# Rotary positions loaded by one transfer on the weights' queue instead of four on GpSimd's

## The chip, the core and the metric

The kernel runs on one core of one Trainium2 chip. The metric is the device time of one execution in microseconds. The engines are named as the profile names them: PE is TensorE (PEld its weight loads), DVE is VectorE, ACT is ScalarE, POOL is GpSimd, and SP issues transfers. An engine name with a q behind it (SPq, POOLq) is that engine's instruction queue.

## What is computed

One decoder layer for 256 tokens of width 2048, in float32: a norm of the input, one wide projection, causal attention with low-rank queries and keys (16 heads), a short gated convolution beside it, two output projections merged by gates, an output projection, a norm and the residual. What the change touches is the rotary table, which turns integer positions into a cosine and a sine for each of 32 frequencies:

```python
def _rope_tables(positions):
    inv_freq = ROPE_THETA ** (-jnp.arange(0, ROPE_DIM, 2, dtype=jnp.float32) / ROPE_DIM)
    ang = positions.astype(jnp.float32)[..., None] * inv_freq
    return jnp.cos(ang), jnp.sin(ang)
...
h = _rmsnorm(x, pre_norm_g)
proj = jnp.einsum('bsd,de->bse', h, w_in)
(q_a, c_kv, k_rope, z_mla, ...) = jnp.split(proj, cuts, axis=-1)
q  = jnp.einsum('bsr,re->bse', _rmsnorm(q_a, q_a_norm_g), w_q_b)
kv = jnp.einsum('bsr,re->bse', _rmsnorm(c_kv, kv_a_norm_g), w_kv_b)
q_rope = _apply_rope(q_rope, cos, sin); k_rope = _apply_rope(k_rope, cos, sin)
```

The positions are 256 consecutive integers from a start below 1024. The rotary parts are first used for the keys and the first heads' queries, after q_a, c_kv and k_rope have been projected.

## The kernel before

**Weights.** All weights come through SP's queue as a list of units, in the order in which TensorE uses them (`plan`, filled by `add`). A unit is one transfer, mostly 1 MB. The first eight (`u_qa`) hold two slices of the transposed input and of the q_a weights each, 768 KB; then come four units of c_kv's weights (`u_ckv`), one of k_rope's (`u_kr`), and those of the gates z, the heads and the output projections. `load_raw` issues a unit's transfer (line 157), the first three units in two transfers each. Units go into three rotating buffers named `raw`, except the fourth to the sixth, which borrow room from `cv_f` and `at_f` so that six units can be on the way at once (`early`, line 298). A unit that reuses a `raw` buffer is issued when the unit before it in that buffer has been split.

**Splitting.** Every float32 operand is split into a high and a low part so that TensorE can multiply at its faster type: ScalarE rounds the high part (`whi`, line 237) and VectorE subtracts it from the source to get the low part (`wlo`, line 238). The eight first units need a scaled copy of the input too, made by ScalarE (line 338) and VectorE (line 341). A product is three matmuls: high by high, and the two crossed ones. All matmuls go through line 88 in program order; those of transposes through line 91.

**Order at the start.** TensorE multiplies q_a (eight units, `qa` in the profile), c_kv (four units, `ckv`), k_rope (`kr`), then the first gate units (`z`), between which the normalised q_a and c_kv are transposed (`lt_qa`, `lt_ckv`, line 484). Beside that, the other engines compute:

- the input norm: ScalarE sums squares of the token-major input (line 351) and GpSimd takes the inverse root with a power (line 358);
- the norms of q_a and c_kv, in the same way, each with its own power on GpSimd and its own scaling on ScalarE (line 475);
- the rotary table, in `tables()`.

**The table.** `tables()` is a generator that is advanced at four places. Its first part loads the positions: four transfers on GpSimd's queue (line 396), each spreading 64 of the 256 positions over 32 partitions, so that the tile `ta_i` holds 128 partitions by 64 positions (frequency by partition). GpSimd converts them (line 407) and reduces the angles exactly into plus or minus pi by 35 small instructions in a row (lines 402 and 405), each reading what the one before wrote. The second part, advanced after the first c_kv unit, clamps the angle on VectorE (line 429) and takes sine and cosine on ScalarE (lines 431 and 432). The third, advanced after the second c_kv unit, copies the results in 32 pieces into `cos_t` and `sin_t` on GpSimd (line 439). The last fixes signs on VectorE (line 442).

**What sets the order.** A planner orders instructions by a timing model, but those inside `keep_in_program_order` keep their written order on their engine. The table's instructions on GpSimd, its clamp and its sine and cosine are kept so, and so are all matmuls. Each engine runs its queue strictly in order: an instruction that waits holds all behind it.

Of the kernel before, what the change touches and what calls it, by code (L numbers as in the profile page):

```python
# [13 lines left out]
I32 = mybir.dt.int32  # L14
# [4 lines left out]
P = 128  # L19
S = 256  # L20
# [20 lines left out]
SQ = S // 4  # L41
# [41 lines left out]
def tile_layer(ctx: ExitStack, tc: tile.TileContext, xw, x, pos, pvec, post_g, wc, wz, wcv, wkr, wqk, wqr, wv, cwr, wsq, out):  # L83
    nc = tc.nc
# [23 lines left out]
    def add(ap, width=UNIT):  # L108
        plan.append((ap, width))
        return len(plan) - 1  # L110


    u_qa = [add(xw[i], 2 * XW) for i in range(KD // 2)]
# [36 lines left out]
    def load_raw(i):  # L150
        ap, w = plan[i]
        t = early.get(i)
        if t is None:
            t = wpool.tile([P, UNIT], F32, name=f"raw{i}", tag="raw", bufs=3)
        cuts = {0: (S, XW, 2 * XW), 1: (0, XW, 2 * XW), 2: (0, XW, 2 * XW)}.get(i, (0, w))
        for a, b in zip(cuts[:-1], cuts[1:]):
            nc.sync.dma_start(out=t[:, a:b], in_=ap[:, a:b])
        raws[i] = t
        if i == u_ckv[1]:
            tc.keep_in_program_order(nc.sync.dma_start(out=x_tok, in_=x))  # L160

    def split_unit(i):
        t, w = raws.pop(i), plan[i][1]
        parts = []
        if i == u_kr:
            t = t[:, :w].rearrange("p (k c) -> p k c", k=KD)
            for h in range(2):
                both = wpool.tile([P, HALF], F32R, name=f"whi{i}_{h}", tag="whi", bufs=5)
                both = both[:, :].rearrange("p (k j c) -> p k j c", k=KD // 2, j=2)
                ks = slice(h * KD // 2, (h + 1) * KD // 2)  # L170
                split_act(both[:, :, 0], both[:, :, 1], t[:, ks])
                parts.append(both.rearrange("p k j c -> p k (j c)"))
            splits[i] = parts
            return
        if i <= u_qa[-1]:

            hi, lo = (wpool.tile([P, HALF], F32R, name=f"{o}{i}", tag=o, bufs=5) for o in ("whi", "wlo"))
            for j in range(2):
                k, o = 2 * i + j, j * XW
                src = x_first if k == 0 else t[:, o : o + S]  # L180
                split_scaled(x_both, src, k)
                split_act(hi[:, j * R : (j + 1) * R], lo[:, j * R : (j + 1) * R], t[:, o + S : o + XW], True)
            splits[i] = [(hi, lo)]
            return
        for h in range(0, w, HALF):
            n = min(HALF, w - h)
            if u_out[3, 0] <= i < u_out[3, 3]:
                hi, lo = (op.tile([P, HALF], F32R, name=f"w{o}{i}_{h}") for o in ("hi", "lo"))
            else:
                hi = wpool.tile([P, HALF], F32R, name=f"whi{i}_{h}", tag="whi", bufs=5)  # L190
                lo = wpool.tile([P, HALF], F32R, name=f"wlo{i}_{h}", tag="wlo", bufs=5)
            split_act(hi[:, :n], lo[:, :n], t[:, h : h + n])
            parts.append((hi, lo))
        splits[i] = parts

    def ahead(i, raw=3, split=1):
        while done["raw"] < min(i + raw, len(plan)):
            load_raw(done["raw"])
            done["raw"] += 1
        while done["split"] < min(i + 1 + split, len(plan)):  # L200
            while done["raw"] <= done["split"]:
                load_raw(done["raw"])
                done["raw"] += 1
            split_unit(done["split"])
            done["split"] += 1

    def take(i):
        ahead(i)
        parts = splits.pop(i)

        def piece(j, n):
            o = j * n
            h, o = o // HALF, o % HALF
            return parts[h][0][:, o : o + n], parts[h][1][:, o : o + n]

        return piece

    def bank(name, tag="mm", bufs=4):
        return psum.tile([P, 512], F32, name=name, tag=tag, bufs=bufs)
# [30 lines left out]
    def col(name, k=0):  # L250
        o, _ = PV[name]
        return pv[:, o + k : o + k + 1]
# [47 lines left out]
    def temp(name, shape=(P, S), dt=F32, bufs=2, tag=None):  # L300

        tag, n = tag or name.rstrip("0123456789_"), shape[-1]
        if n % LINE == 0:
            return bp.tile(list(shape), dt, name=name, tag=tag, bufs=bufs)
        return bp.tile([P, -(-n // LINE) * LINE], dt, name=name, tag=tag, bufs=bufs)[:, :n]
# [83 lines left out]
        nc.vector.tensor_tensor(dst, dst, r_x[:, :], op=ALU.mult)  # L389


    def tables():

        pi = temp("ta_i", (P, SQ), I32, 1)
        for q in range(4):
            nc.gpsimd.dma_start(
                out=pi[32 * q : 32 * q + 32, :], in_=pos[:, SQ * q : SQ * (q + 1)].to_broadcast([32, SQ])
            )
        y, n1, n2, r = (temp(f"ta_{n}", (P, SQ), bufs=1) for n in "ymnr")

        def scale(*a, **kw):
            tc.keep_in_program_order(nc.gpsimd.tensor_scalar(*a, **kw))

        def minus(*a):
            tc.keep_in_program_order(nc.gpsimd.tensor_tensor(*a, op=ALU.subtract))

        tc.keep_in_program_order(nc.gpsimd.tensor_copy(y[:, :], pi[:, :]))
        scale(r[:, :], y[:, :], col("freq"), None, op0=ALU.mult)

        def less(r, n, c):  # L410

            scale(y[:, :], n[:, :], c, None, op0=ALU.mult)
            minus(r[:, :], r[:, :], y[:, :])

        inv = 1.0 / (2.0 * math.pi)
        big, small = 1.5 * 2.0**38, 1.5 * 2.0**23
        scale(y[:, :], r[:, :], inv, None, op0=ALU.mult)
        scale(n1[:, :], y[:, :], big, big, op0=ALU.add, op1=ALU.subtract)
        minus(n2[:, :], y[:, :], n1[:, :])
        scale(n2[:, :], n2[:, :], small, small, op0=ALU.add, op1=ALU.subtract)  # L420
        for w, c in TERMS:
            less(r, (n1, n2)[w], c)
        scale(n1[:, :], r[:, :], inv, small, op0=ALU.mult, op1=ALU.add)
        scale(n1[:, :], n1[:, :], small, None, op0=ALU.subtract)
        for c in COARSE:
            less(r, n1, c)
        yield
        lim = float(np.nextafter(np.float32(math.pi), np.float32(0)))
        tc.keep_in_program_order(nc.vector.tensor_scalar(r[:, :], r[:, :], lim, -lim, op0=ALU.min, op1=ALU.max))
        nc.vector.scalar_tensor_tensor(y[:, :], r[:, :], -1.0, r[:, :], op0=ALU.mult, op1=ALU.max)  # L430
        tc.keep_in_program_order(nc.scalar.activation(n2[:, :], r[:, :], AF.Sin))
        tc.keep_in_program_order(nc.scalar.activation(n1[:, :], y[:, :], AF.Sin, bias=hpi[:, :], scale=-1.0))
        yield

        for o in range(4):
            for q in range(4):
                to, ti = slice(32 * o, 32 * o + 32), slice(32 * q, 32 * q + 32)
                for dst, src in ((cos_t, n1), (sin_t, n2)):
                    tc.keep_in_program_order(nc.gpsimd.tensor_copy(dst[to, SQ * q : SQ * (q + 1)], src[ti, :]))
        yield  # L440
        tc.keep_in_program_order(
            nc.vector.tensor_scalar(sin_t[:, :], sin_t[:, :], col("sign"), None, op0=ALU.mult)
        )
        yield
# [11 lines left out]
    def latent_products(pss, k, w, wk):  # L456
        cols = [x_both[:, k, o : o + P] for o in (0, P, S, S + P)]
        wh, wl_ = w(wk, R)
        for i, ws, first, last in ((0, wh, True, False), (2, wh, False, False), (0, wl_, False, True)):
            for t in range(NT):  # L460
                matmul(
                    pss[t][:, :], cols[i + t], ws, start=first and k == 0, stop=last and k == KD - 1
                )
# [13 lines left out]
    def latent_turn(name, both, g, tags):  # L477
        f = lat_f[name]
        for j2 in range(2):
# [5 lines left out]
            for j in range(2):  # L485
# [4 lines left out]
                )  # L490

    table_parts = tables()
    next(table_parts)
    ps_q = [bank(f"qa{t}") for t in range(NT)]
    for i in range(KD // 2):
        ahead(u_qa[i], raw=3 + len(early), split=0)
        w = take(u_qa[i])
        for j in range(2):
            latent_products(ps_q, 2 * i + j, w, j)
# [584 lines left out]
```

## Time and profile before

| | |
|---|---|
| median of 3 runs | 1038.01 us (1038.0 to 1038.07) |
| profiled execution | 1039.19 us |
| its span | 1037.4 us |
| granted TensorE clock | 0.998 |
| busy: PE, DVE, ACT, POOL | 1027.2, 682.3, 526.6, 181.0 us |
| SP's queue (q1) | 197.54 MB |
| GpSimd's queue (q0) | 29.38 MB |

The times in the profile start at the span's first instruction, and the span is 1.8 us shorter than the execution's time. In a row of the timeline the first number is the start, the second the length (of a merged group, from the first start to the last end), then engine, line, operation, what is written and read, and how many; the bracket tells how long the engine stood idle before it and what ended the wait. In the DMA view the last number is the time from a transfer's issue to its landing, and the share of a queue is that of all 16 DMA engines' time. In the chain by time the rows are start, length and what ran.

### The profile page before, as it was taken

The numbers are of one execution on the slowest core, as the hardware profiler recorded it, in microseconds if no ns is written. First come the engines' busy times: TensorE is split into PE (matmuls) and PEld (weight loads), VectorE is DVE, ScalarE is ACT, GpSimd is POOL, SyncE is SP. The second block draws the span as 40 slices with busy tenths as digits, with TensorE's granted clock in tenths as the row PEclk, the third lists the DMA queues.
The fourth block names the chain that finished last, engine by engine and source line by source line (L and its number), as shares of the span: only waits on it lengthen the run. The fifth ranks groups of instructions, "written<-read, shape, count | busy, mean of one in ns | idle before, by whom it ended". The sixth has DMA issues, their size and how long they took to land.

```text
span 1037.4 us, 12723 instructions
## 1 busy us (share of the span) xinstructions
PE 1027.2 (99%) x4694; PEld 856.3 (83%) x4694; DVE 682.3 (66%) x954; ACT 526.6 (51%) x733; POOL 181.0 (17%) x345
## 2 busy tenths in 40 slices
PE   9999999999999999999999999999999999999996
PEld 7888888888888888888888888888888888888885
DVE  7579777787687786767777785564465455455562
ACT  7767555555555455554554564444334434443551
POOL 7620321114211232212313120020010001002000
PEclk9999999999999999999999999999999999999999
DMA  8745766568565685757676766565555566558642
GB/s 323 304 175 215 232 213 234 193 222 295 190 250 202 219 282 189 272 210 243 236 262 200 261 228 212 183 228 198 203 203 209 197 203 236 181 191 331 235 165 82
DMA packets 41952, 231.04 MB, mean 223 GB/s; under 512 B 7521, under 2 KB 8225, under 8 KB 18977
## 3 DMA queue, kind: packets, MB, share of 16 engines
q1 hardware_dynamic: 29808, 197.54, 53.9%
q0 software_dynamic: 11648, 29.38, 8.5%
q10 hardware_dynamic: 432, 3.29, 0.8%
q8 instruction: 37, 0.61, 0.2%
q14 instruction: 27, 0.21, 0.1%
HBM read 214.48 MB, written 11.53 MB: 218 GB/s over the span
## 4 chain that ended last, share of the span: by engine, by line
PE 98%; DMA 1%; DVE 0%; ACT 0%; SPq 0%; DVEq 0%; issue 0%
PE cv L88 34%; PE sq L88 34%; PE z L88 8%; PE out L88 8%; PE qn L88 2%; PE kn L88 2%; PE vv L88 2%; PE ckv L88 2%; PE qa L88 2%; PE sc L88 1%; PE qr L88 1%; PE o L88 1%; DMA raw<-xw_dram 1%; PE kr L88 0%; DVE og L971 0%; PE lt_qa L91 0%
## 5 line engine op out<-in xcount | busy, mean ns | idle before, releaser
L238 DVE TENSOR_TENSOR wlo<-raw,whi 128x1024 fp32r<-128x1024 f32 (+1 forms) x370 | 441.1, 1198 | 284.1 <-ACT whi L237 273.9
L237 ACT ACTIVATE whi<-raw 128x1024 fp32r<-128x1024 f32 (+1 forms) x372 | 382.9, 1035 | 396.2 <-PE sq L88 180.5
L88 PE MATMUL cv<-whi,x_both 128*128 128x512 f32 x1024 | 321.1, 389 | 0.0
L88 PEld LDWEIGHTS cv<-whi,x_both 128*128 128x128 f32 x1024 | 192.3, 188 | 39.2
L88 PE MATMUL cv<-wlo,x_both 128*128 128x512 f32 x512 | 199.5, 390 | 0.0
L88 PE MATMUL sq<-whi,x_both 128*128 128x512 f32 x512 | 158.3, 389 | 0.0
L88 PEld LDWEIGHTS sq<-whi,x_both 128*128 128x128 f32 x512 | 96.1, 188 | 19.9
L88 PEld LDWEIGHTS cv<-wlo,x_both 128*128 128x128 f32 x512 | 96.2, 188 | 19.0
L88 PE MATMUL sq<-wlo,x_both 128*128 128x512 f32 x256 | 99.6, 389 | 0.0
L88 PE MATMUL z<-whi,x_both 128*128 128x512 f32 x256 | 80.6, 390 | 0.0
L88 PE MATMUL sq<-whi,at_both 128*128 128x512 f32 x256 | 79.5, 389 | 0.0
L88 PE MATMUL sq<-whi,cv_both 128*128 128x512 f32 x256 | 79.4, 389 | 0.0
L88 PE MATMUL out<-whi,m_both 128*128 128x512 f32 x256 | 78.9, 389 | 0.0
L319 POOL DMA_DIRECT2D far<-sg x32 | 17.5, 555 | 312.2 <-DVE sg L312 238.6
L319 POOL DMA_DIRECT2D far<-via x64 | 35.4, 560 | 195.1 <-DVE via L312 194.7
L88 PEld LDWEIGHTS sq<-wlo,x_both 128*128 128x128 f32 x256 | 48.0, 188 | 10.0
L88 PEld LDWEIGHTS z<-whi,x_both 128*128 128x128 f32 x256 | 48.1, 188 | 9.9
L88 PEld LDWEIGHTS sq<-whi,at_both 128*128 128x128 f32 x256 | 48.0, 188 | 9.9
L88 PEld LDWEIGHTS out<-whi,m_both 128*128 128x128 f32 x256 | 48.0, 188 | 9.9
L88 PEld LDWEIGHTS sq<-whi,cv_both 128*128 128x128 f32 x256 | 48.0, 188 | 9.9
L88 PE MATMUL z<-wlo,x_both 128*128 128x512 f32 x128 | 49.8, 389 | 0.0
L88 PE MATMUL sq<-wlo,at_both 128*128 128x512 f32 x128 | 49.8, 389 | 0.0
(214 smaller groups left out, 1128.0 us busy)
## 6 DMA issues: line engine op xcount, KB each, us to landing
raw<-wsq_dram SPq DMA_DIRECT2D x80, 1024.0 KB, 4.7
raw<-wcv_dram SPq DMA_DIRECT2D x64, 1024.0 KB, 5.8
raw<-wz_dram SPq DMA_DIRECT2D x16, 1024.0 KB, 4.7
raw<-wqk_dram SPq DMA_DIRECT2D x8, 1024.0 KB, 5.1
cw<-cwr_dram POOLq DMA_DIRECT2D x24, 256.0 KB, 6.2
raw<-wc_dram SPq DMA_DIRECT2D x4, 1024.0 KB, 9.9
raw<-wv_dram SPq DMA_DIRECT2D x4, 1024.0 KB, 4.7
far<-via POOLq DMA_DIRECT2D x64, 48.0 KB, 3.3
```

Source lines behind the costliest of these rows:

```text
L88: return tc.keep_in_program_order(nc.tensor.matmul(*a, **kw))
L237: a = nc.scalar.activation(hi, src, AF.Copy)
L238: b = nc.vector.tensor_tensor(lo, src, hi.bitcast(F32), op=ALU.subtract)
L319: tc.keep_in_program_order(nc.gpsimd.dma_start(out=f[i], in_=m))
```

## The change

The positions are laid out in the input array as the tile needs them: 128 rows of 64 integers, each group of 64 positions repeated over 32 rows, instead of one row of 256. One transfer on SP's queue loads all of them, issued directly behind the sixth unit of the plan and ahead of the seventh, and kept in that place in program order. The four transfers on GpSimd's queue are gone. The tile is made ahead of `tables()`, and the generator's first part is now advanced after the first six units have been issued. What is computed from the tile is unchanged.

As compiled, every engine has the same instructions in the same order as before, except that GpSimd loses the four transfers and SP's queue gains one.

```diff
@@ load_raw
         raws[i] = t
+        if i == u_qa[5]:
+            tc.keep_in_program_order(nc.sync.dma_start(out=tables_pi, in_=pos))
         if i == u_ckv[1]:
             tc.keep_in_program_order(nc.sync.dma_start(out=x_tok, in_=x))
@@ tables
+    tables_pi = temp("ta_i", (P, SQ), I32, 1)
+
     def tables():
 
-        pi = temp("ta_i", (P, SQ), I32, 1)
-        for q in range(4):
-            nc.gpsimd.dma_start(
-                out=pi[32 * q : 32 * q + 32, :], in_=pos[:, SQ * q : SQ * (q + 1)].to_broadcast([32, SQ])
-            )
+        pi = tables_pi
@@ the q_a stage
     table_parts = tables()
-    next(table_parts)
     ps_q = [bank(f"qa{t}") for t in range(NT)]
     for i in range(KD // 2):
         ahead(u_qa[i], raw=3 + len(early), split=0)
+        if i == 0:
+            next(table_parts)
         w = take(u_qa[i])
@@ the arrays made on the host
-        "pos": arr(positions).reshape(1, S),
+        "pos": np.repeat(arr(positions).reshape(4, SQ), 32, axis=0),
```

## The prediction

> **What bounds the kernel now.** I read the page's busy shares first, then the chain by time for the opening, the DMA view, and the timeline of each engine up to 60 us.
>
> ```profile
> span 1037.4 us, 12723 instructions
> ...
> PE 1027.2 (99%) x4694; PEld 856.3 (83%) x4694; DVE 682.3 (66%) x954; ACT 526.6 (51%) x733; POOL 181.0 (17%) x345
> ```
>
> TensorE is the bound and is busy for 99% of the span. So a saving elsewhere buys almost nothing, and whatever makes TensorE wait costs its full length.
>
> ```profile
> 1.64 6.58 DMA raw<-xw_dram
> ...
> 9.33 19.38 PE qa L88 x84
> 28.71 21.76 PE ckv L88 x96
> ```
>
> The chain by time: a transfer releases the second unit's work, and from 9.33 us on it is TensorE alone: qa, then ckv (four units of four k's), then kr. The change touches the inputs of the table that ScalarE and VectorE make beside this stretch.
>
> ```profile
> at_f<-xw_dram SPq DMA_DIRECT2D x1, 768.0 KB, 11.8
> ...
> ta_i<-pos_dram POOLq DMA_DIRECT2D x4, 8.0 KB, 6.1
> ```
> ```profile
> 1.80 2.16 POOL L396 DMA_DIRECT2D ta_i<-pos_dram  x4
> ...
> 4.76 0.43 SPq L157 DMA_DIRECT2D at_f<-xw_dram  x1
> ...
> 7.03 4.37 SPq L157 DMA_DIRECT2D raw<-xw_dram  x2
> ...
> 9.93 0.24 POOL L407 CAST ta_y<-ta_i 128x64 f32<-128x64 int32 x1 [5.03 <-DMA ta_i<-pos_dram]
> ...
> 10.27 1.02 POOL L402 TENSOR_SCALAR ta_r<-ta_y,pv 128x64 f32<-128x64 f32 x1
> ...
> 13.44 0.60 POOL L405 TENSOR_TENSOR ta_n<-ta_y,ta_m 128x64 f32<-128x64 f32 x1
> ...
> 15.91 0.86 POOL L405 TENSOR_TENSOR ta_r<-ta_r,ta_y 128x64 f32<-128x64 f32 x1
> ...
> 16.86 0.42 POOL L402 TENSOR_SCALAR ta_y<-ta_m 128x64 f32<-128x64 f32 x1
> ...
> 24.61 1.22 POOL L402 TENSOR_SCALAR ta_y<-ta_n 128x64 f32<-128x64 f32 x1
> ...
> 29.52 1.10 POOL L402 TENSOR_SCALAR ta_m<-ta_r 128x64 f32<-128x64 f32 x1
> ...
> 30.70 0.38 POOL L402 TENSOR_SCALAR ta_m<-ta_m 128x64 f32<-128x64 f32 x1
> ...
> 33.35 0.32 POOL L405 TENSOR_TENSOR ta_r<-ta_r,ta_y 128x64 f32<-128x64 f32 x1
> ```
>
> GpSimd's range reduction: a cast at 9.93, then 35 dependent instructions from 10.27 to 33.35 + 0.32 = 33.67. It is the only long thing between the positions and the sine.
>
> ```profile
> 33.94 0.26 ACT L431 ACTIVATE ta_n<-ta_r 128x64 f32<-128x64 f32 x1 [3.69 <-DVE ta_r L429]
> ...
> 34.66 2.01 ACT L237 ACTIVATE whi<-raw 128x1024 fp32r<-128x1024 f32 x2
> ...
> 41.50 4.18 ACT L237 ACTIVATE whi<-raw 128x1024 fp32r<-128x1024 f32 x5
> ```
> ```profile
> 33.95:45.65 11.70, 11.70 (x53) 9.68 (x52) 6.60 (x14) 11.51 (x18) 3.94 (x5) 1.00 0.54 212
> ```
>
> ScalarE already stands idle for 3.69 us before the sine (L431), which is kept in program order. Behind it stand the splits of ckv's third unit (34.66), the squares of the input norm and, at 41.50, the splits of ckv's fourth unit. From 33.94 to 45.68 (41.50 + 4.18) ScalarE has no gap to speak of (the stretch's row: length, then busy us of PE, PEld, DVE, ACT and POOL; ACT 11.51 of 11.70), so a late sine moves all of this by the same amount.
>
> **The change part by part.**
>
> *The four GpSimd issues go* (2.16 us from 1.80). Behind them stand only mask instructions, needed by the first scores, long after; GpSimd idled 5.03 us for the positions anyway. Worth nothing.
>
> *Their packets leave the first 10 us of DMA.*
>
> ```profile
> q1 hardware_dynamic: 860, 2.96, 94.9%
> q0 software_dynamic: 128, 0.03, 2.8%
> ```
>
> Between 4 and 12 us (the DMA view of that stretch) the four transfers took 2.8% of 8 us = 0.22 us. The second unit may land up to that much earlier, so TensorE may start at 9.1 for 9.33: a gain of 0 to 0.22 us, which the next step swallows if TensorE waits later.
>
> *One issue on SP's queue behind the sixth unit.* SP issues it at about 5.2 (4.76 + 0.43), in the gap before the seventh unit's at 7.03; about 0.4 us, free. In the compiled program the transfers take eight completion counters in turn, so one more makes the seventh unit's issue wait for the second unit's first piece. The chain above has that piece land at 1.64 + 6.58 = 8.2. The seventh unit is queued behind units that land up to 16.56, so an issue at 8.2 is not late; with the positions' 128 rows ahead of it, it lands some 0.2 later, and TensorE takes it up only after 22 us (five units of 2.72 us from 9.33; 2.72 is half of 21.76/4). Free.
>
> *The positions land later: this carries the price.* At 5.2 us the queue holds most of six units. The sixth (at_f) landed 4.76 + 11.8 = 16.56, and the positions stand behind it. Their own 0.22 us are balanced by the 0.22 taken out ahead. I take 16.56 + 0.15 (landing to cast in the profile: the last of the old four, issued near 3.46, landed by 9.8, cast 9.93) = 16.7 for the cast, not 9.93: 6.8 us late. Bounds: 16.5 (with the sixth unit) and 17.2 (0.5 us of their own).
>
> *How much of 6.8 us reaches the sine.* The pace of the 35 instructions depends on what VectorE does beside them:
>
> ```profile
> 10.97 0.47 DVE L341 SCALAR_TENSOR_TENSOR x_both<-raw,pv,x_both 128x256 fp32r<-128x256 f32 x1
> 11.36 0.68 DVE L238 TENSOR_TENSOR wlo<-raw,whi 128x512 fp32r<-128x512 f32 x1
> ...
> 17.62 0.54 DVE L341 SCALAR_TENSOR_TENSOR x_both<-at_f,pv,x_both 128x256 fp32r<-128x256 f32 x1
> 18.08 0.72 DVE L238 TENSOR_TENSOR wlo<-at_f,whi 128x512 fp32r<-128x512 f32 x1
> ...
> 23.62 3.16 DVE L238 TENSOR_TENSOR wlo<-raw,whi 128x512 fp32r<-128x512 f32 x3
> ...
> 28.03 2.49 DVE L238 TENSOR_TENSOR wlo<-raw,whi 128x1024 fp32r<-128x1024 f32 x2 [1.25 <-ACT whi L237]
> ```
>
> Slow pace: from 10.27 to 16.86, 7 instructions, 0.94 us each; each that overlaps a 0.68 us subtraction (L238) ends just after it. Quick pace: from 16.86 to 24.61, 14 instructions, 0.55 each, two for each VectorE pair, which stretches a little (0.47 to 0.54, 0.68 to 0.72). From 24.61 to 30.70, beside the wide subtractions, 7. Then, with VectorE waiting, 7 from 30.70 to 33.67: 0.43 each.
>
> In the changed kernel the first starts at 16.7 + 0.34 (10.27 - 9.93) = 17.04, so 7.6 us are left up to 24.61. The quick pace set in where a two-input subtraction (L405) alternates with a scale (L402); the first four (three scales, then a subtraction) are not such, and in the profile the step from first to fourth took (13.44 - 10.27)/3 = 1.06 each. So four take 4.2 us (to 21.3) and the rest of the stretch holds 3.3/0.55 = 6: ten done by 24.61, 17 by 30.70. The other 18 run at 0.43 us while VectorE and ScalarE both wait for them: 7.7 us, ready at 38.4 instead of 33.67, so the sine is 4.7 us late. Ends: all quick, 13 + 7 done, 15 left, 37.15 (3.5 late); all slow, 8 + 7, 20 left, 39.3 (5.6 late).
>
> The Trainium skill, "SBUF — State Buffer", section "Who interferes with whom", says that a VectorE instruction with two SBUF inputs and a GpSimd one that reads SBUF hold one port pair by turns, the second to issue blocked until the first ends. By that rule a GpSimd instruction loses at most the rest of one subtraction and then has its turn, two fit each VectorE pair from the start, and the sine would be 3.5 us late. The rows agree only from 16.86 on; from 10.27 the turns went one to a pair.
>
> *What of 4.7 us reaches TensorE.*
>
> ```profile
> 39.20 0.87 PEld L88 LDWEIGHTS ckv<-whi,x_both 128*128 128x128 f32 x4
> ...
> 42.58 1.22 DVE L238 TENSOR_TENSOR wlo<-raw,whi 128x1024 fp32r<-128x1024 f32 x1 [0.26 <-ACT whi L237]
> ...
> 45.55 0.41 PEld L88 LDWEIGHTS ckv<-wlo,x_both 128*128 128x128 f32 x2
> ```
>
> The third ckv unit's high part is split by 34.66 + 1.0 = 35.66 and taken at 39.20: slack 3.5. The fourth unit's low part is ready at 43.80 and taken at 45.55: slack 1.75, less 0.05 from an end to a start, 1.7. That is the least, so TensorE ends 4.7 - 1.7 = 3.0 us later: about 1.2 us of wait at the third unit, the rest at the fourth. The possible 0.22 us at the start is inside this, since the sine's time does not hang on TensorE. Nothing later gives it back: TensorE has no other gap.
>
> *What is late next.*
>
> ```profile
> 42.40 0.70 POOL L358 TENSOR_TENSOR r_qa<-v_qa,mhalf 128x2 f32<-128x2 f32 x1 [0.94 <-DVE v_qa L471]
> ...
> 57.83 0.69 POOL L358 TENSOR_TENSOR r_ckv<-v_ckv,mhalf 128x2 f32<-128x2 f32 x1
> ...
> 58.80 1.27 ACT L475 ACTIVATE at_f<-ckv,r_ckv 128x512 f32<-128x512 f32 x2 [3.07 <-DVE r_ckv L473]
> ...
> 63.45 1.04 PE L91 MATMUL lt_ckv<-ident,at_f 128*128 128x128 f32 x8
> ```
>
> The 32 table copies run on GpSimd between these two powers, and the second power, which the ckv norm needs, stands behind them. They move by 4.7, TensorE by 3.0. The scaled ckv is there at 60.07 and transposed at 63.45, a slack of 3.4, which falls to 1.7. It holds unless the copies, which now lie otherwise to VectorE's work, take over 1.7 us more.
>
> **Sum.** 1039.19 us (the profiled execution: span 1037.4, 1.8 outside) + 3.0 = 1042.2. The median of the three runs is 1.18 lower, so 1038.01 + 3.0 = 1041.0 us. About 0.2% (2.1 us) is what a measurement can tell from no change.
>
> **Rivals.**
> 1. *Quick pace from the start:* sine 3.5 late, TensorE 3.5 - 1.7 = 1.8 late, 1039.8 us, within 0.2%. For it: fourteen instructions in a row went so. Against: the first seven, the same instructions beside the same kind of pair, did not. Beside it stands the rule of "SBUF — State Buffer" in the Trainium skill told above.
> 2. *Not slower: the table is hidden anyway.* The sine must be ready within 1.7 us of now, 33.67 + 1.7 = 35.4. With 0.43 us each after 30.70 only 11 may be left, so 17, not ten, must be done between 17.04 and 24.61: 0.45 us each, the unhindered pace. Then the saved packets alone count: 1037.8 to 1038.0 us. Against: no stretch with VectorE busy shows that pace.
> 3. *The copies become the wait:* 1 us or so beyond the 1.7, about 1042 us. For it: single copies between 0.23 and 1.29 us, by VectorE's work:
>
> ```profile
> 43.85 1.29 POOL L439 COPY sin_t<-ta_n 32x64 f32<-32x64 f32 x1
> ...
> 50.71 0.23 POOL L439 COPY sin_t<-ta_n 32x64 f32<-32x64 f32 x1
> ```
>
> **How the numbers follow.** Forecast (TensorE 2.1 to 3.9 us later) 0.75; rival 1 0.13; rival 3 0.08; rival 2 0.04. The predicted time is 1041.0. Range: from rival 1 with the earliest landing (0.2 us less), 1039.6, to the slow end, 1038.01 + 5.6 - 1.7 = 1041.9, and 0.9 for a landing at 17.2 and a part of rival 3: 1042.8. Slower by over 0.2%: 0.75 + 0.08 = 0.83. Within 0.2%: rival 1 and three quarters of rival 2, 0.16. Faster: 0.01, since TensorE's wait before 9.33 is the only one to win back.
>
> **What the profile of the changed kernel would show.** The cast (L407) near 16.7 instead of 9.93, else the landing is wrong. The last subtraction before VectorE's clamp ending near 38.4 and ScalarE's idle time before the sine growing from 3.69 to about 8.4, else the pace is wrong. TensorE's first idle time after 9.3, at ckv, about 1 us at the third unit and 2 at the fourth, released by ScalarE's and VectorE's splits; if it is absent, the slack was misread. No new wait at the transposes of ckv. From kr on, all of TensorE's work should stand 3.0 us later by a constant. A transfer that passes the units, a quick pace, or a wait in the copies would make the number wrong.

## The result and the profile after

The changed kernel takes 1041.64 us (median of 7 runs, 1041.17 to 1042.07) against 1038.07 us for the kernel before beside it (7 runs): 3.57 us more, a ratio of 1.0033 with a 95% interval of 1.0023 to 1.0043. It is slower by more than the 0.2% that can be told from no change. The profiled execution took 1041.41 us with a span of 1039.6 us. In `kernel.py` of the changed kernel the splits stand at lines 239 and 240, the first power at 360.

The head of its page, and then the waits of TensorE and of its weight loads in ckv (us in total, times, the longest):

```profile
span 1039.6 us, 12717 instructions
...
PE 1028.1 (99%) x4694; PEld 856.0 (82%) x4694; DVE 681.9 (66%) x954; ACT 526.4 (51%) x733; POOL 177.5 (17%) x341
```
```profile
PE ckv L88 <- ACT whi L239: 2.6, 2, 1.8
...
PEld ckv L88 <- DVE wlo L240: 1.0, 2, 0.5
```

TensorE's busy time is the same within 0.9 us. What is new is that it waits for ScalarE twice in ckv, 2.6 us together, and that its weight loads wait twice for VectorE's low parts, 1.0 us together. The page still calls TensorE 99% busy: a share says nothing of 3 us in 1040. The timeline of GpSimd and of the engines behind it tells where they come from:

```profile
4.54 0.43 SPq L157 DMA_DIRECT2D at_f<-xw_dram  x1
5.01 0.43 SPq L160 DMA_DIRECT2D ta_i<-pos_dram  x1
...
15.38 0.92 POOL L407 CAST ta_y<-ta_i 128x64 f32<-128x64 int32 x1 [12.62 <-DMA ta_i<-pos_dram]
16.40 1.04 POOL L402 TENSOR_SCALAR ta_r<-ta_y,pv 128x64 f32<-128x64 f32 x1
...
19.59 0.79 POOL L405 TENSOR_TENSOR ta_n<-ta_y,ta_m 128x64 f32<-128x64 f32 x1
...
30.28 0.37 POOL L402 TENSOR_SCALAR ta_y<-ta_n 128x64 f32<-128x64 f32 x1
...
37.58 0.32 POOL L405 TENSOR_TENSOR ta_r<-ta_r,ta_y 128x64 f32<-128x64 f32 x1
```
```profile
27.13 1.28 ACT L431 ACT_TABLE_LOAD   x1
38.16 0.26 ACT L431 ACTIVATE ta_n<-ta_r 128x64 f32<-128x64 f32 x1 [9.74 <-DVE ta_r L429]
...
38.73 1.99 ACT L239 ACTIVATE whi<-raw 128x1024 fp32r<-128x1024 f32 x2
```
```profile
39.83 1.20 PE L88 MATMUL ckv<-whi,x_both 128*128 128x512 f32 x4 [1.84 <-ACT whi L239]
...
46.66 1.20 PE L88 MATMUL ckv<-whi,x_both 128*128 128x512 f32 x4 [0.73 <-ACT whi L239]
...
52.58 3.79 PE L88 MATMUL kr<-x_both,whi 128*128 128x512 f32 x16
```

The positions are issued at 5.01 us, at once behind the sixth unit, and GpSimd gets them 15.3 us into the span. The last of the 35 instructions ends at 37.90; ScalarE, done with its table load at 28.4, waits 9.74 us for the sine and only then splits the third ckv unit. TensorE stands still for that split and again for the fourth unit's, which stands behind it on ScalarE.

One thing does not fit this tale yet: kr begins at 52.58 here and began at 50.30 in the first profile of the kernel before, a difference of 2.3 us and not of 3.6. TensorE did not wait for the second unit in this profile, as it had for 1.24 us in the first profile of before. The first experiment is for that.

### The profile page after: what moved, and what is told of

Read it like the earlier page. It is cut to its first block, busy times and chain, and to the rows that moved or that the text cites. A ratio compares the mean times of both kernels' runs of the same rounds, so it can differ in the third digit from the quotient of the medians.

```text
span 1039.6 us, 12717 instructions
## 1 busy us (share of the span) xinstructions
PE 1028.1 (99%) x4694; PEld 856.0 (82%) x4694; DVE 681.9 (66%) x954; ACT 526.4 (51%) x733; POOL 177.5 (17%) x341
## 4 chain that ended last, share of the span: by engine, by line
PE 95%; POOL 2%; issue 2%; ACT 1%; DVE 0%; DVEq 0%; ACTq 0%; POOLq 0%
PE cv L88 34%; PE sq L88 33%; PE z L88 8%; PE out L88 8%; PE qn L88 2%; PE kn L88 2%; PE vv L88 2%; PE sc L88 1%; PE qr L88 1%; PE o L88 1%; POOL ta_y L402 1%; POOL ta_r L405 1%; PE ckv L88 0%; PE kr L88 0%; ACT whi L239 0%
## 6 DMA issues: line engine op xcount, KB each, us to landing
raw<-wc_dram SPq DMA_DIRECT2D x4, 1024.0 KB, 10.6
```

## The experiments

Each ratio is that of the run's median to the kernel before in executions beside it (1038.17 or 1038.2 us), with its 95% interval.

**The kernel before, once more.** No edit.

> The kernel before, unchanged, profiled once more. In the first profile TensorE waited 1.24 us for the second unit and began its unbroken work at 9.33 us; in the changed kernel it did not wait there and stood 1.4 us earlier at the same matmul. Theory S1: the four GpSimd transfers slow the second unit, so here TensorE waits about 1.2 us again and begins near 9.3. Theory S2: the landing of the second unit differs from run to run, so here it begins near 8 and the span is about 1036.3 instead of 1037.4. Time by both: 1038.0 to 1038.2.

Measured: 1037.93 us against 1038.17 (ratio 0.9999, 0.9989 to 1.0008), span 1035.9. TensorE goes on with the second unit's products at 8.00, and its only wait in the span is the one at its start:

```profile
PE idle L88 <- POOL hpi L261: 1.1, 1, 1.1
```
```profile
33.05 0.26 ACT L431 ACTIVATE ta_n<-ta_r 128x64 f32<-128x64 f32 x1 [3.44 <-DVE ta_r L429]
```
```profile
48.80 3.79 PE L88 MATMUL kr<-x_both,whi 128*128 128x512 f32 x16
```

S2 held: the late second unit belongs to that one execution and not to the four GpSimd transfers, which are in this kernel too. This execution, at 1037.68 us, is like the others of the kernel before; the first profile's 1039.19 is longer than any of them on record (the longest is 1038.97). An ordinary execution of the kernel before thus has kr at 48.8, and against that the changed kernel's 52.58 is 3.8 us late, close to the 3.57 of the medians. Why the second unit landed late in the first profile stays open.

**The changed kernel, once more.** No edit.

> The changed kernel, unchanged, profiled once more beside the runs above. Theory A: TensorE waits 1.8 us and 0.7 us at the third and fourth ckv unit again, and some tenths for the low parts; kr begins near 52.5 us, 3.6 later than in a kernel without the wait; 1041.2 to 1042.1 us. If TensorE stands idle at the second unit in this profile, the span grows by less than that idle time, since the sine does not depend on TensorE.

Measured: 1041.65 us (ratio 1.0035, 1.0023 to 1.0048). The sine starts at 38.32, TensorE waits 1.92 and 0.72 us, kr begins at 52.75. The two profiles agree within 0.2 us at each step.

**The transfer ahead of all units.**

```diff
 def load_raw(i):
     ap, w = plan[i]
+    if i == u_qa[0]:
+        tc.keep_in_program_order(nc.sync.dma_start(out=tables_pi, in_=pos))
...
-    if i == u_qa[5]:
-        tc.keep_in_program_order(nc.sync.dma_start(out=tables_pi, in_=pos))
```

> The changed kernel with the positions' transfer ahead of the first unit on the same queue, everything else as changed. Theory A (the positions come too late, the sine holds ScalarE, TensorE waits at ckv): cast near 4 to 5 us, range reduction done by 31 us, no wait of ScalarE before the sine beyond 1 us, no TensorE wait at ckv, 1038.0 to 1038.6 us (the first unit's issue is 0.4 us later). Theory B (128 rows of 256 bytes on the weights' queue hold up the units, wherever they stand): 1041 us or more.

Measured: 1038.77 us (ratio 1.0006, 0.9997 to 1.0015), 0.2 above the range of theory A and far from B. In the profile the cast starts at 2.82, the sine at 30.63 after 0.28 us of waiting, and TensorE has no wait at ckv. It waits 0.43 us for the second unit instead, and kr begins at 49.85. So the 128 short rows and their issue ahead of all units cost 0.6 us in the median, which the interval does not tell from nothing; how much of that is the issue and how much the rows was not parted. What costs 3.6 us is the place behind the units.

**The transfer on ScalarE's queue.**

```diff
+    tc.keep_in_program_order(nc.scalar.dma_start(out=tables_pi, in_=pos))
...
-    if i == u_qa[5]:
-        tc.keep_in_program_order(nc.sync.dma_start(out=tables_pi, in_=pos))
```

> The changed kernel with the positions' transfer on ScalarE's queue, behind that of the per-partition vectors and not behind the weights. Theory A: cast between 5 and 8 us, range reduction done before 32 us, no TensorE wait at ckv, 1037.5 to 1038.2 us. Theory B: the units have their queue to themselves again, so about 1038 as well; with the run above this tells A and B apart.

Measured: 1038.19 us (ratio 1.0000, 0.9990 to 1.0009). The cast starts at 5.41, the sine at 29.80, no wait at ckv. So early a sine buys nothing, since ScalarE then waits for the third ckv unit itself:

```profile
33.85 2.01 ACT L237 ACTIVATE whi<-raw 128x1024 fp32r<-128x1024 f32 x2 [3.38 <-DMA raw<-wc_dram]
```

Without GpSimd's four transfers and without a late table the time is that of the kernel before: taking the four transfers away gains nothing that can be measured.

**The transfer behind the third unit, and behind the fifth.** Each is one digit:

```diff
-        if i == u_qa[5]:
+        if i == u_qa[2]:   # in the other run: u_qa[4]
```

> The changed kernel with the transfer behind the third unit instead of the sixth. Theory A: landing near 10 us (the sixth unit's 15.3 less three units of 1.8), cast near 10, sine near 34 as in the kernel before, slack just kept or short by up to 0.7 us: 1037.8 to 1038.8 us. Theory B: 1041 us or more, as behind the sixth.

> The changed kernel with the transfer behind the fifth unit instead of the sixth. Theory A: cast near 13.5 us; between the third unit's case (cast 9.33, sine 32.39) and the sixth's (15.38, 38.16) that gives a sine near 36.4; each us of sine beyond about 34.5 costs one: 1.9 us more than before, 1039.3 to 1040.6 us. If a step and not a slope: 1038 or 1041.6.

Measured: 1037.72 us behind the third (ratio 0.9997, 0.9988 to 1.0007), 1039.83 us behind the fifth (1.0016, 1.0007 to 1.0025). The first lies 0.1 under its range, and its sine came 1.6 us earlier than expected; the second is as expected. Behind the third:

```profile
9.33 0.90 POOL L407 CAST ta_y<-ta_i 128x64 f32<-128x64 int32 x1 [6.58 <-DMA ta_i<-pos_dram]
```
```profile
32.39 0.26 ACT L431 ACTIVATE ta_n<-ta_r 128x64 f32<-128x64 f32 x1 [3.70 <-DVE ta_r L429]
```
```profile
48.76 3.79 PE L88 MATMUL kr<-x_both,whi 128*128 128x512 f32 x16
```

and behind the fifth:

```profile
36.31 0.26 ACT L431 ACTIVATE ta_n<-ta_r 128x64 f32<-128x64 f32 x1 [8.00 <-DVE ta_r L429]
```
```profile
44.82 1.20 PE L88 MATMUL ckv<-whi,x_both 128*128 128x512 f32 x4 [0.73 <-ACT whi L239]
...
50.74 3.79 PE L88 MATMUL kr<-x_both,whi 128*128 128x512 f32 x16
```

From the fifth to the sixth the sine moves by 38.16 - 36.31 = 1.85 us and kr by 52.58 - 50.74 = 1.84: one for one. With kr at 48.75, as behind the third unit and in the kernel before once more, the line meets it at a sine of 36.31 - (50.74 - 48.75) = 34.3 us. Up to there a later sine is free; beyond it each us costs one. The point is worked out and not measured: no run has its sine between 33.05 and 36.31, and the start of a single execution shifts it by some tenths (on ScalarE's queue kr began at 49.30 without a wait at ckv, its first unit having taken 0.5 us longer). The kernel before, with its sine at 33.05 in an ordinary execution, is 1.25 us away from that point.

**A shorter chain.**

```diff
-        for w, c in TERMS:
+        for w, c in TERMS[:4]:
```

> The changed kernel with 4 of the 11 terms of the first reduction instead of all (14 of GpSimd's 35 instructions fewer; the angles are then reduced less exactly, so the table is not the reference's). The transfer, its place and every other instruction stay. Theory A (the late sine holds ScalarE): 14 x 0.43 = 6.0 us off the chain, sine near 32.1 instead of 38.2, no TensorE wait at ckv, 1037.8 to 1038.4 us. Theory B (the late transfer itself, or what it does to the units): 1041 us or more, as with all terms.

Measured: 1037.91 us (ratio 0.9999, 0.9989 to 1.0008). The positions come as late as in the changed kernel (cast at 15.19), but the sine starts at 31.90 and no wait is left:

```profile
31.90 0.26 ACT L431 ACTIVATE ta_n<-ta_r 128x64 f32<-128x64 f32 x1 [3.67 <-DVE ta_r L429]
```
```profile
48.68 3.79 PE L88 MATMUL kr<-x_both,whi 128*128 128x512 f32 x16
```

So the late landing itself harms nothing. The seventh unit is not issued later either: at 6.88 here and 6.80 in the changed kernel, against 7.05 in the kernel before once more. The whole price passes through the time at which the sine's argument is ready.

**The sine later in ScalarE's order.**

```diff
-        if i == 0:
-            next(table_parts)
         if i == 1:
             dg = input_norm()
             latent_norm("qa", ps_q)
-            next(table_parts)
+        if i == 2:
+            next(table_parts)
+            next(table_parts)
```

> The changed kernel with the clamp, sine and cosine written behind the third ckv unit instead of the first; positions as late as in the changed kernel, chain of the same length. Theory A (ScalarE's order turns the late table into a wait of TensorE): no TensorE wait at the third and fourth ckv units; the copies still begin after 45 us and end after 60, so the scaled ckv comes at 61 to 63 us, when an undisturbed TensorE wants to transpose it at 62: a wait of 0 to 1.5 us there; 1038.0 to 1039.6 us. Theory C (the wait comes from GpSimd's and VectorE's port, not from ScalarE's order): 1041 us or more.

Measured: 1039.98 us in the median (ratio 1.0021, 1.0012 to 1.0031), a little above the range. The planner moved some work of the norm of ckv with it. ScalarE splits the ckv units without a stop, and TensorE reaches kr at 48.53, the earliest of all; the wait at ckv is gone, though GpSimd's chain ends at 39.72, later than in the changed kernel, which refutes theory C. But the copies now begin at 48.66 (47.10 in the changed kernel), and the power of the ckv norm stands behind them and ends at 61.93. VectorE then first finishes a split and a piece of qa and starts the norm's last step at 62.84, where in the changed kernel it followed the power at once. So the scaled ckv is late at the transposes:

```profile
PE lt_ckv L91 <- ACT at_f L475: 2.5, 2, 2.2
```

In this profile the wait cost more than itself. The windows around it: length, busy us of TensorE, its weight loads, VectorE, ScalarE and GpSimd, then the granted clock, the DMA share and GB/s:

```profile
63.00:64.00 1.00, 0.00 (x0) 0.00 (x0) 0.87 (x2) 1.00 (x3) 0.00 (x0) 1.00 0.00 0
64.00:65.00 1.00, 0.69 (x4) 0.50 (x5) 0.02 (x1) 0.95 (x3) 0.00 (x0) 1.00 0.00 0
65.00:66.00 1.00, 1.00 (x8) 0.96 (x7) 0.73 (x2) 0.78 (x2) 0.00 (x0) 0.84 0.00 0
66.00:67.00 1.00, 1.00 (x4) 0.72 (x4) 0.90 (x3) 0.89 (x3) 0.00 (x0) 0.50 0.00 0
67.00:68.00 1.00, 1.00 (x4) 0.81 (x3) 0.97 (x4) 0.16 (x1) 0.00 (x0) 0.50 0.00 0
68.00:69.00 1.00, 1.00 (x4) 0.82 (x3) 0.80 (x2) 0.88 (x1) 0.00 (x0) 0.50 0.00 0
69.00:70.00 1.00, 1.00 (x5) 0.77 (x5) 0.79 (x1) 0.18 (x1) 0.00 (x0) 0.95 0.00 0
```

After the idle 2.2 us the granted clock fell to 0.50. The 0.84 and the 0.95 put this between about 65.7 and 69.1 us; 3.4 us at half the clock cost 1.7, by that estimate. This execution took 1041.86 us. One other of the ten took 1042.38; the other eight lie between 1039.34 and 1040.44. That those eight kept their clock is a guess: their mean clocks over the execution, 0.997 to 0.999 against 0.996 and 0.997 for the two long ones, lie too close together to tell.

## Why the prediction was right, point by point

The forecast was 1041.0 us, 3.0 more than before, and the measured 1041.64 is 3.57 more. Direction, mechanism and place held. Against an ordinary execution two terms of the sum were too favourable, the lateness of the sine by 0.4 us and the slack by 0.45, and the sine's forecast time was in part luck.

- *The four issues and their packets: worth nothing.* Right. The possible 0.22 us at the start does not show: with the four transfers (the kernel before once more) TensorE had no wait for the second unit to win back.
- *One issue on SP's queue: free.* Right. The seventh unit's issue did not move to 8.2: it came at 6.80, at once behind the split of the first unit (end at 6.77), whose buffer it takes.
- *The landing.* The cast was put at 16.7 and came at 15.38. The step itself held: the sixth unit landed 10.6 us after its issue at 4.54, 15.1, and the positions 10.3 after 5.01, 15.3, so 0.2 us behind it. The sixth unit had landed at 16.56, 1.4 us later, in the profile that I counted from, the one with the late second unit.
- *The pace: the sum held, the parts only in part.* The first four instructions went as forecast, 1.06 us from one to the next ((19.59 - 16.40)/3), and the last at 0.43 us. Between them the quick pace of 0.55 us hardly came: the fifth to the ninth took 0.74 us each ((24.15 - 20.46)/5). Two things made up for it. VectorE was done with its subtractions at 28.69 and not at 30.5, so that the last pace set in at 29.00, and 18 of 35 were done by 30.7 where I had 17. And the landing was 1.3 us early, of which a cast of 0.92 us instead of 0.24 took half. The sine came at 38.16; 33.94 + 4.7 = 38.6 was forecast, and that the two are so close is in part luck. The quick pace from the start, rival 1, did not come. By my reading of the rule on the shared port pair in the Trainium skill, "SBUF — State Buffer", section "Who interferes with whom", it would have. The trace agrees with it only in part: beside VectorE's subtraction the first scale took 1.04 us, and with the transfer ahead of the units, where the same scale met no subtraction, it took 0.51 us; but the turns went one to a VectorE pair for the first four, not two.
- *The slack of 1.7 us, and what it is counted from: this is what was mis-sized.* It was read at the fourth unit's low part in an execution whose TensorE had lost 1.24 us at the second unit. In that execution TensorE stood 1.5 us later than in an ordinary one (kr at 50.30 for 48.80) and the sine 0.9 (33.94 for 33.05), which made the slack look larger. The runs put the point at a sine of 34.3; from the 33.05 of an ordinary execution that is 1.25 us, and the sine was 5.1 us late against it (38.16 - 33.05), not 4.7. So 5.1 - 1.25 = 3.85 for kr (48.80 to 52.58 is 3.78), for a forecast 4.7 - 1.7 = 3.0; the medians differ by 3.57. That the median of before lay 1.2 us under its profiled execution was on view, and it was the sign that the profile's start was not the usual one.
- *The division between the units.* I had 1.2 us at the third unit and the rest at the fourth; measured are 1.84 and 0.73 us for the high parts, and about 0.5 us in each unit for the low parts. So more of it falls on the third unit than forecast, whose slack was read in the same execution.
- *What is late next: nothing.* Right. The scaled ckv of the changed kernel is ready at 64.2 and is transposed at 65.73; 1.5 us are left where I had 1.7. The 32 copies took 14.8 us (47.10 to 61.90) for 14.7 before, so rival 3 did not come. The sine written later showed how near this is: there it was the wait.
- *Rival 2, a hidden table,* is what stands behind the third unit or on ScalarE's queue; behind the sixth it fails for the reason given: the unhindered 0.43 us came only from 29.00 on, when VectorE was waiting.

## What to carry to other kernels

Follow a small late input through its chain to the first engine that waits for it in program order: what counts is when the chain's end is wanted, and what the waiting instruction holds up behind it. Here a place in a queue cost the landing of everything ahead of it, so a small input of a long chain goes on another queue or far ahead: behind the third large transfer it was free, behind the fifth it cost 1.6 us. Before counting slack in a profile, compare its time with the median, and mistrust a profile whose start is not that of the other runs.

## What was not expected of the hardware

In the profile with the later sine the granted clock fell to 0.50 from about 65.7 to 69.1 us, behind a TensorE wait of 2.2 us and two short bursts of transposes, while waits of 1.84 and 0.73 us in the changed kernel left it at 1.00. The Trainium skill, "TensorE: Matmul & The Clock Gate", Part 1, says that the clock falls back after an idle window of about 3.4 us. No stretch here without any TensorE instruction is that long; the one without a product, from 61.83 to 65.38, is 3.55 us, with eight transposes in it. Whether transposes keep the clock up no run here shows, so this trace neither bears the figure out nor refutes it.
